# Accumulating layer 0's later modulation groups on VectorE instead of TensorE

## The chip, the core and the metric

The kernel runs on one core of a Trainium2 chip: TensorE (PE), VectorE (DVE), ScalarE (ACT), GpSimd (POOL), and SyncE (SP), which issues the DMA transfers. The metric is the device time of one execution in microseconds.

## What is computed

A backbone of two layers runs over 256 context and 256 latent tokens of width 1024, all in float32. Each layer begins by making six modulation vectors for each of the two streams from a conditioning vector and a 1024 x 6144 matrix. This is the part that the change touches:

```python
c_act = jax.nn.silu(c)
cc_act = jax.nn.silu(c_ctx)
for l in range(DEPTH):
    m_l = jnp.split((c_act @ w_ada[l] + b_ada[l])[:, None, :], 6, axis=-1)
    m_c = jnp.split((cc_act @ w_ada[l] + b_ada[l])[None, None, :], 6, axis=-1)
    h_l = modulate(rms_norm(x, norm_g[l, 0]), m_l[0], m_l[1])
    h_c = modulate(rms_norm(ctx, norm_g[l, 0]), m_c[0], m_c[1])
    y_l, y_c = token_mixer(h_l, h_c, ...)
    x = x + m_l[2] * rms_norm(y_l, norm_g[l, 1])
    h_l = modulate(rms_norm(x, norm_g[l, 2]), m_l[3], m_l[4])
    x = x + m_l[5] * rms_norm(sq_relu_mlp(h_l, w_mlp_up[l], w_mlp_down[l]), norm_g[l, 3])
    ...
```

The token mixer has three branches: a gated linear recurrence (four heads), differential attention (four heads) and windowed attention; each is projected, gated and summed. The product of a vector with w_ada is small arithmetic (two rows), but w_ada is 25 MB per layer and has to pass through some engine.

## The kernel before

Activations are kept transposed in `h`, as a high and a low part in fp32r; each weight block (512 KB twice) is loaded into a ring `raw`, and `weights` (L196) splits it: ScalarE copies the high part (L226), VectorE subtracts it for the low part (L227), into one of two buffers `whl`. A block is consumed by three dense matmuls for each tile (L248 to L250 with tokens as the stationary side, L260 to L262 with weights). At the end of each `weights` call `self.pump(self.rate)` (L229) takes that many closures off the list `pumps` and runs them: this is how the modulation work is spread among the weight blocks.

The six vectors of a layer are computed in three groups of 2048 columns. Group 0 of layer 0 is needed at once and is done at the start, in `first_blocks` (L535). Groups 1 and 2 of layer 0 are queued by `ada_queue`: 16 steps for each group, in which one slice of w_ada, 128 rows by 1024 columns (half of each of four strips), is loaded and multiplied on TensorE by `CA`, which holds both streams in a stationary tile of 32 columns. Four matmuls (L364) go to four column strips of the array and accumulate over eight steps in PSUM bank 7, which is kept for that. `ada_done` (L428) copies the bank out (L433), transposes it (L437) and adds the bias (L443). Layer 1's groups are computed in another way, by `ada_late` while layer 0's MLP runs: VectorE multiplies each slice by its per-partition factor and accumulates it in SBUF, one accumulator per stream (L400, L403); after eight slices TensorE sums over the partitions by four matmuls with `ones` per stream (L412), and the result is copied (L417), transposed (L420) and given its bias (L426).

What sets the order: the program is recorded in source order, and a scheduler with its own timeline places the instructions on each engine's queue; splits and evacuations have high priority, closures run at ordinary priority behind the last weight load (`issue_after`). Each engine's queue then keeps its order. PSUM has eight banks: two for dense outputs (`dps`), the others in rotation for the rest (`mps`), without bank 7 in layer 0's mixers. The helper names in the rows: L795 to L869 are the recurrence heads, L949 to L1036 the differential-attention heads (L949 and L950 scores, L989 to L995 their normalisation on VectorE, L1001 transposes, L1014 values), L1087 to L1122 the windowed attention. The buffers named `arf` are units of 512 columns in one arena.

Of the kernel before, what the change touches and what calls it, by code (L numbers as in the profile page):

```python
# [14 lines left out]
ALU = mybir.AluOpType  # L15
# [96 lines left out]
class Net:  # L112
    def __init__(self, ctx, tc, ins, out):
# [40 lines left out]
        self.rate = 1  # L154
# [198 lines left out]
    def ada_queue(self, l, g):  # L353
        for half in range(2):
            for k in range(8):
                self.pumps.append(lambda half=half, k=k: self.ada_step(l, g, half, k))
        self.pumps.append(lambda: self.ada_done(l, g))

    def ada_step(self, l, g, half, k):
        nc = self.nc  # L360
        ca = self.CA.rearrange("p (k m) -> p k m", m=32)
        raw = self.ada_load(l, g, half, k)
        for j in range(4):
            nc.tensor.matmul(self.ps[7][32 * j:32 * j + 32, half * 256:half * 256 + 256], ca[:, k, :],  # L364
                             raw[:, j * 256:(j + 1) * 256], start=k == 0, stop=k == 7)
        raw.free()

    def ada_late(self, l, groups, ahead=2):

        todo = [(g, half, k) for g in groups for half in range(2) for k in range(8)]  # L370
        raws, acc = [], []

        def step(n):
            while len(raws) < min(n + 1 + ahead, len(todo)):
                raws.append(self.ada_load(l, *todo[len(raws)]))
            g, half, k = todo[n]
            self.ada_acc(raws[n], k, acc, 1 if l == DEPTH - 1 and g else 2)
            if k == 7:
                self.ada_sum(l, g, half, acc)
                acc.clear()  # L380

        self.pumps += [lambda n=n: step(n) for n in range(len(todo))]

    def ada_load(self, l, g, half, k):
        src = self.I["w_ada"][l][k * 128:k * 128 + 128, g * 2048:(g + 1) * 2048]
        src = src.rearrange("p (j h c) -> p j h c", j=4, h=2)[:, :, half, :]
        raw = self.A.get(2)
        with self.tc.issue_after(self.last_dma.ins):
            self.nc.sync.dma_start(raw[:, :].rearrange("p (j c) -> p j c", j=4), src)
        return raw  # L390

    def ada_acc(self, raw, k, acc, streams):

        ca = self.CA.rearrange("p (k m) -> p k m", m=32)
        if k == 0:
            acc += [self.A.get(2) for _ in range(streams)]
# [10 lines left out]
    def ada_sum(self, l, g, half, acc):  # L407
        nc = self.nc
        ps = self.mps()
        for s, a in enumerate(acc):  # L410
            for j in range(4):
                nc.tensor.matmul(ps[32 * j:32 * j + 32, s * 256:s * 256 + 256], self.ones[:, 0:32],  # L412
                                 a[:, j * 256:j * 256 + 256], start=True, stop=True)
            a.free()
        t = self.A.get(1)
        n = 2 * len(acc)
# [5 lines left out]
        qs = slice(2 * half, 2 * half + 2)  # L422
        out = self.M[l].rearrange("p (s g j q) -> p s g j q", s=2, g=3, j=4)[:, :, g, :, qs]
        bb = self.bT[:, l * 48 + g * 16:l * 48 + g * 16 + 16].rearrange("p (j q) -> p j q", j=4)[:, :, qs]
        for s in range(len(acc)):
            nc.vector.tensor_tensor(out=out[:, s], in0=view(p2, s * 256, [(32, 4), (128, 2)]), in1=bb, op=ALU.add)  # L426
# [253 lines left out]
    def hgrn_dense(self, l, w, hp):  # L680
# [560 lines left out]
    def layer(self, l):  # L1241
# [140 lines left out]
    def build(self):  # L1382
        self.setup()
        for g in (1, 2):
            self.ada_queue(0, g)
# [30 lines left out]
```

## Time and profile before

| | |
|---|---|
| median of 3 runs | 1603.66 us (1602.57 to 1603.8) |
| the profiled execution | 1602.47 us, its span 1600.7 us |
| TensorE matmul, weight load | busy 97%, 83% of the span |
| VectorE, ScalarE, GpSimd | busy 65%, 49%, 25% |
| DMA | 220.06 MB, 137 GB/s on average |

The page gives busy time by engine over the whole span; the views below cut the span in stretches, follow single instructions on one engine in order of time, or group instructions by source line. A matmul's end is modelled, so the distance from start to start tells what a matmul costs its engine, and busy time tells more than it takes. Each fp32 matmul appears as two records.

### The profile page before, as it was taken

Reading aid. Unit: us, or ns where it says so; the run is one execution under the profiler, and the core shown is the slowest. Engines: PE = TensorE matmul, PEld = TensorE weight load, DVE = VectorE, ACT = ScalarE, POOL = GpSimd, SP = SyncE. Lnnn points to the kernel's source line nnn. Section 1 sums busy time; section 2 is a strip of 40 time slices with the busy share of each in tenths; the row PEclk is TensorE's granted clock in tenths of the full one; section 3 lists DMA queues with packets and bytes.
Section 4 is the critical chain, followed back from the end, with each engine's and each line's share of the span. In section 5 each row is a group of like instructions: output and inputs, shape, how many; then the busy total and the mean of one; then the engine's idle time right before and its main releaser. Section 6 shows DMA issues by size and latency. Waiting matters only on the chain.

```text
span 1600.7 us, 26956 instructions
## 1 busy us (share of the span) xinstructions
PE 1546.6 (97%) x10326; PEld 1323.4 (83%) x10326; DVE 1045.6 (65%) x1897; ACT 777.4 (49%) x1588; POOL 393.0 (25%) x419
## 2 busy tenths in 40 slices
PE   6999999999999999999999999999898999989997
PEld 4788887878777778888888888999897999889996
DVE  3655544577477568777656546786668788665665
ACT  4443433446444457533424246644445656666553
POOL 1142415050420001210102011464455250121001
PEclk9999999999999999999999999999999999999999
DMA  9823234233332336466566434432334254446562
GB/s 282 236 80 119 75 114 143 80 79 115 123 93 79 115 109 211 140 202 194 176 208 191 151 106 145 125 114 78 122 106 106 67 149 125 148 139 191 185 185 92
DMA packets 209681, 220.06 MB, mean 137 GB/s; under 512 B 24400, under 2 KB 177168, under 8 KB 209552
## 3 DMA queue, kind: packets, MB, share of 16 engines
q1 hardware_dynamic: 209552, 218.34, 45.2%
q8 instruction: 81, 1.33, 0.3%
q14 instruction: 48, 0.39, 0.1%
HBM read 217.26 MB, written 1.05 MB: 136 GB/s over the span
## 4 chain that ended last, share of the span: by engine, by line
PE 85%; DVE 5%; POOL 4%; DMA 2%; ACT 2%; issue 2%; SPq 1%; POOLq 0%; DVEq 0%; ACTq 0%
PE b L248 16%; PE b L249 16%; PE b L250 16%; PE b L260 8%; PE b L261 8%; PE b L262 8%; POOL arf L919 1%; PE b L364 1%; DVE whl L227 1%; PE b L1122 1%; PE b L1109 1%; PE b L869 1%; PE b L949 1%; PE b L950 1%; PE b L853 1%
## 5 line engine op out<-in xcount | busy, mean ns | idle before, releaser
L227 DVE TENSOR_TENSOR whl<-raw,whl 128x512 fp32r<-128x512 f32 x588 | 431.4, 753 | 243.3 <-ACT whl L226 233.7
L226 ACT CAST whl<-raw 128x512 fp32r<-128x512 f32 x588 | 356.3, 620 | 256.4 <-PE b L262 129.3
L248 PE MATMUL b<-h,whl 128*128 128x512 f32 (+1 forms) x1296 | 447.6, 347 | 1.2 <-ACT arf L964 0.6
L250 PE MATMUL b<-h,whl 128*128 128x512 f32 (+1 forms) x1296 | 444.9, 344 | 0.8 <-DVE whl L227 0.8
L249 PE MATMUL b<-h,whl 128*128 128x512 f32 (+1 forms) x1296 | 444.6, 343 | 0.4 <-POOL h L606 0.3
L248 PEld LDWEIGHTS b<-h,whl 128*128 128x128 f32 x1296 | 247.9, 192 | 33.8 <-ACT whl L226 2.9
L250 PEld LDWEIGHTS b<-h,whl 128*128 128x128 f32 x1296 | 246.8, 191 | 29.5 <-issue 1.6
L249 PEld LDWEIGHTS b<-h,whl 128*128 128x128 f32 x1296 | 246.9, 191 | 28.9 <-issue 2.4
L1332 POOL TENSOR_TENSOR arf<-arf 128x256 f32<-128x256 f32 (+1 forms) x68 | 59.8, 880 | 411.3 <-ACT arr L1331 399.5
L262 PE MATMUL b<-whl,arr 128*128 128x512 f32 x384 | 149.9, 390 | 0.0
L261 PE MATMUL b<-whl,arr 128*128 128x512 f32 x384 | 149.9, 390 | 0.0
L260 PE MATMUL b<-whl,arr 128*128 128x512 f32 x384 | 149.7, 391 | 0.0
L919 POOL TENSOR_TENSOR arf<-arf,cst 32x256 f32<-32x256 f32 x104 | 94.3, 907 | 192.3 <-ACT arf L964 70.7
L260 PE MATMUL b<-whl,h 128*128 128x256 f32 (+1 forms) x416 | 129.0, 313 | 0.0
L261 PE MATMUL b<-whl,h 128*128 128x256 f32 (+1 forms) x416 | 128.7, 311 | 0.0
L262 PE MATMUL b<-whl,h 128*128 128x256 f32 (+1 forms) x416 | 128.6, 311 | 0.0
L455 POOL TENSOR_TENSOR sm<-sm,nhalf 128x1 f32<-128x1 f32 (+2 forms) x42 | 37.0, 883 | 333.5 <-DVE sm L630 242.5
L809 POOL TENSOR_TENSOR arf<-arf 128x512 f32<-128x512 f32 x56 | 75.8, 1376 | 43.7 <-ACT arf L788 24.1
L260 PEld LDWEIGHTS b<-whl,h 128*128 128x128 f32 x416 | 80.0, 192 | 6.4 <-ACT arf L753 0.8
L260 PEld LDWEIGHTS b<-whl,arr 128*128 128x128 f32 x384 | 72.1, 188 | 15.9 <-issue 1.2
L262 PEld LDWEIGHTS b<-whl,arr 128*128 128x128 f32 x384 | 72.1, 188 | 14.9
L261 PEld LDWEIGHTS b<-whl,arr 128*128 128x128 f32 x384 | 72.1, 188 | 14.5
(224 smaller groups left out, 2434.1 us busy)
## 6 DMA issues: line engine op xcount, KB each, us to landing
raw<-in_w_in_dram SPq DMA_DIRECT2D x110, 512.0 KB, 3.9
arf<-in_w_ada_dram SPq DMA_DIRECT2D x80, 512.0 KB, 4.9
raw<-in_w_mlp_down_dram SPq DMA_DIRECT2D x72, 512.0 KB, 3.8
raw<-in_w_mlp_up_dram SPq DMA_DIRECT2D x64, 512.0 KB, 4.3
raw<-in_w_out_dram SPq DMA_DIRECT2D x24, 512.0 KB, 4.2
arf<-in_w_ada_dram SPq DMA_DIRECT2D x32, 256.0 KB, 5.6
raw<-in_w_branch_dram SPq DMA_DIRECT2D x16, 512.0 KB, 3.9
raw<-in_w_in_dram SPq DMA_DIRECT2D x32, 128.0 KB, 3.3
```

The costliest lines, as they stand in the source:

```text
L226: self.behind(ops, lambda: nc.scalar.copy(r32(h), src))
L227: self.split_op = self.behind(ops, lambda: nc.vector.tensor_tensor(out=r32(l), in0=src, in1=h, op=ALU.subtract))
L248: nc.tensor.matmul(ps, wh, xh[:, t0:t0 + n], start=start and k == 0, stop=False)
L249: nc.tensor.matmul(ps, wh, xl[:, t0:t0 + n], start=False, stop=False)
L250: nc.tensor.matmul(ps, wl, xh[:, t0:t0 + n], start=False, stop=stop and k == nk - 1)
L260: nc.tensor.matmul(ps, xh, wh, start=start and k == 0, stop=False)
L261: nc.tensor.matmul(ps, xh, wl, start=False, stop=False)
L262: nc.tensor.matmul(ps, xl, wh, start=False, stop=stop and k == nk - 1)
L455: self.nc.gpsimd.tensor_tensor(out=r, in0=ms, in1=self.nhalf[:, 0:cols], op=ALU.pow)
L809: nc.gpsimd.tensor_tensor(out=kx, in0=kx, in1=view(cur, 1, [(nb - 1, 2), (2, nb // 2), (0, h)]), op=ALU.mult)
L919: nc.gpsimd.tensor_tensor(out=b[o, 0:LAT], in0=x[i], in1=self.cst[i, C_RS:C_RS + LAT], op=ALU.mult)
L1332: nc.gpsimd.tensor_tensor(out=r[:, c], in0=r[:, c], in1=r[:, c], op=ALU.mult)
```

## The change

Layer 0's groups 1 and 2 now go through `ada_late` too, in quarters of 512 columns; two closures run per weight block instead of one, so that the same 1024 columns pass per block. `ada_queue` and `ada_step` are gone. Bank 7 joins the rotation after `first_blocks`. Layer 1's slices, still 1024 columns, are now consecutive columns instead of half of each strip.

```diff
-        self.rate = 1
+        self.rate = 2
...
-    def ada_queue(self, l, g):
-        for half in range(2):
-            for k in range(8):
-                self.pumps.append(lambda half=half, k=k: self.ada_step(l, g, half, k))
-        self.pumps.append(lambda: self.ada_done(l, g))
-
-    def ada_step(self, l, g, half, k):
...
-        raw = self.ada_load(l, g, half, k)
-        for j in range(4):
-            nc.tensor.matmul(self.ps[7][32 * j:32 * j + 32, half * 256:half * 256 + 256], ca[:, k, :],
-                             raw[:, j * 256:(j + 1) * 256], start=k == 0, stop=k == 7)
...
-    def ada_late(self, l, groups, ahead=2):
+    def ada_late(self, l, groups, cols, ahead=2):
 
-        todo = [(g, half, k) for g in groups for half in range(2) for k in range(8)]
+        todo = [(g, c0, k) for g in groups for c0 in range(0, 2048, cols) for k in range(8)]
         raws, acc = [], []
 
         def step(n):
             while len(raws) < min(n + 1 + ahead, len(todo)):
-                raws.append(self.ada_load(l, *todo[len(raws)]))
+                raws.append(self.ada_load(l, cols, *todo[len(raws)]))
...
-    def ada_load(self, l, g, half, k):
-        src = self.I["w_ada"][l][k * 128:k * 128 + 128, g * 2048:(g + 1) * 2048]
-        src = src.rearrange("p (j h c) -> p j h c", j=4, h=2)[:, :, half, :]
-        raw = self.A.get(2)
+    def ada_load(self, l, cols, g, c0, k):
+        c0 += g * 2048
+        raw = self.A.get(cols // UNIT)
         with self.tc.issue_after(self.last_dma.ins):
-            self.nc.sync.dma_start(raw[:, :].rearrange("p (j c) -> p j c", j=4), src)
+            self.nc.sync.dma_start(raw[:, :], self.I["w_ada"][l][k * 128:k * 128 + 128, c0:c0 + cols])
...
-    def ada_sum(self, l, g, half, acc):
+    def ada_sum(self, l, c0, cols, acc):
+
         nc = self.nc
         ps = self.mps()
+        w, nb = cols // 4, cols // 512
         for s, a in enumerate(acc):
             for j in range(4):
-                nc.tensor.matmul(ps[32 * j:32 * j + 32, s * 256:s * 256 + 256], self.ones[:, 0:32],
-                                 a[:, j * 256:j * 256 + 256], start=True, stop=True)
+                nc.tensor.matmul(ps[32 * j:32 * j + 32, s * w:s * w + w], self.ones[:, 0:32],
+                                 a[:, j * w:j * w + w], start=True, stop=True)
             a.free()
         t = self.A.get(1)
-        n = 2 * len(acc)
+        n = nb * len(acc)
...
+            self.np = 8
             self.setup_mixers()
...
-            self.ada_late(1, range(3))
+            self.ada_late(1, range(3), 1024)
             self.rate = 0
...
-        for g in (1, 2):
-            self.ada_queue(0, g)
+        self.ada_late(0, (1, 2), 512)
```

How the order moves. In the changed kernel the lines lie 13 to 16 lower: L387 and L384 are the former L403 and L400, L398 the former L412, L406 the former L420, L936, L937, L976, L982, L988 and L1001 the former L949, L950, L989, L995, L1001 and L1014, L840 and L856 the former L853 and L869.

The first place is TensorE at the end of the recurrence of layer 0's first head pair. Before:

```order
L853 MATMUL b_86<-arf 128x256 x4
L869 MATMUL b_88<-arf 128x128 x2
L869 MATMUL b_87<-arf 128x128 x6
L869 MATMUL b_88<-arf 128x128 x3
L364 MATMUL b_91<-arf,CA 32x256 x3
L869 MATMUL b_88<-arf 128x128 x6
L364 MATMUL b_91<-arf,CA 32x256 x9
L249 MATMUL b_85<-h,whl 128x512
```

and in the changed kernel:

```order
L840 MATMUL b_86<-arf 128x256 x4
L856 MATMUL b_87<-arf 128x128 x2
L856 MATMUL b_88<-arf 128x128 x4
L856 MATMUL b_87<-arf 128x128 x6
L856 MATMUL b_88<-arf 128x128 x7
L398 MATMUL b_91<-arf,ones 32x128 x8
L248 MATMUL b_85<-h,whl 128x512
```

The steps of four matmuls with 256 columns are gone, and the first of the eight sums, with 128 columns, stands there instead.

The second place is VectorE in the middle of the differential attention. Before, while the heads run:

```order
L992 RECIPROCAL sm<-sm 128x2
L993 TENSOR_SCALAR arf<-arf,sm,lam 128x512
L995 SCALAR_TENSOR_TENSOR arf<-arf,sm 128x512
L992 RECIPROCAL sm<-sm 128x2
L993 TENSOR_SCALAR arf<-arf,sm,lam 128x512
L227 TENSOR_TENSOR whl<-raw,whl 128x512
L995 SCALAR_TENSOR_TENSOR arf<-arf,sm 128x512
L227 TENSOR_TENSOR whl<-raw,whl 128x512
```

and in the changed kernel, at the change from the first head pair to the second:

```order
L976 TENSOR_REDUCE sm<-b_90 128x1
L917 TENSOR_TENSOR arr<-arf,arr 64x512
L387 SCALAR_TENSOR_TENSOR arf<-arf,CA 128x512
L976 TENSOR_REDUCE sm<-b_89 128x1
L982 SCALAR_TENSOR_TENSOR arf<-arf,sm 128x512
L387 SCALAR_TENSOR_TENSOR arf<-arf,CA 128x512
L979 RECIPROCAL sm<-sm 128x2
L917 TENSOR_TENSOR arr<-arf,arr 64x512
L980 TENSOR_SCALAR arf<-arf,sm,lam 128x512
```

The accumulations (L387) stand between the steps of a head's normalisation; 17 of the 128 new VectorE instructions lie between the first L976 and the last L982 of layer 0.

The third place is TensorE towards the end of the same heads. Before:

```order
L248 MATMUL b_84<-h,whl 128x512
L249 MATMUL b_84<-h,whl 128x512
L949 MATMUL b_88<-arr 128x512
L950 MATMUL b_88<-arr 128x512
L250 MATMUL b_84<-h,whl 128x512
L949 MATMUL b_89<-arr 128x512
L1001 MATMUL b_90<-cst,arf 128x128 x4
L950 MATMUL b_89<-arr 128x512
L248 MATMUL b_84<-h,whl 128x512
L249 MATMUL b_84<-h,whl 128x512
```

and in the changed kernel:

```order
L988 MATMUL b_89<-cst,arf 128x128 x2
L936 MATMUL b_88<-arr 128x512
L937 MATMUL b_88<-arr 128x512
L936 MATMUL b_86<-arr 128x512
L937 MATMUL b_86<-arr 128x512
L936 MATMUL b_87<-arr 128x512
L937 MATMUL b_87<-arr 128x512
L1001 MATMUL b_91<-arf 128x128 x4
L936 MATMUL b_88<-arr 128x512
L937 MATMUL b_88<-arr 128x512
L1001 MATMUL b_86<-arf 128x128 x2
```

The dense matmuls that stood between the heads' steps there now stand behind them: from layer 0's first scores to the last transposes of its heads the order has 340 dense matmuls, and 391 before.

## Rows read from the trace of the kernel before

**Rows 1.** The page, part 1: busy us, share of the span, instructions, by engine.

```profile
PE 1546.6 (97%) x10326; PEld 1323.4 (83%) x10326; DVE 1045.6 (65%) x1897; ACT 777.4 (49%) x1588; POOL 393.0 (25%) x419
```

**Rows 2.** The page, part 4: shares of the chain that ended last, by engine.

```profile
PE 85%; DVE 5%; POOL 4%; DMA 2%; ACT 2%; issue 2%; SPq 1%; POOLq 0%; DVEq 0%; ACTq 0%
```

**Rows 3.** Stretches (us): length; PE, PEld, DVE, ACT, POOL busy; clock; DMA; GB/s.

```profile
50.00:600.00 550.00, 542.91 (x3829) 441.54 (x3819) 332.23 (x666) 245.32 (x510) 133.13 (x142) 1.00 0.37 108
289.00:404.00 115.00, 111.19 (x619) 93.05 (x618) 81.88 (x159) 57.43 (x136) 23.15 (x26) 0.99 0.35 95
```

**Rows 4.** Waits of TensorE, 50 to 600 us: total us, times, longest.

```profile
PE b L795 <- DVE arf L812: 2.7, 4, 1.2
PE b L364 <- DMA arf<-in_w_ada_dram: 1.5, 2, 1.3
```

**Rows 5.** Timeline of TensorE: start, length (us), line, tile, records.

```profile
71.37 0.39 PE L249 MATMUL b<-h,arr 128*128 128x512 f32 x1
71.59 0.39 PE L250 MATMUL b<-h,arr 128*128 128x512 f32 x1
71.91 0.64 PE L364 MATMUL b<-arf,CA 128*32 128x256 f32 x8
72.48 0.39 PE L260 MATMUL b<-whl,h 128*128 128x256 f32 x1
72.70 0.28 PE L261 MATMUL b<-whl,h 128*128 128x256 f32 x1
```

**Rows 6.** TensorE by line: records, busy us, mean ns, idle before.

```profile
L364 PE MATMUL b<-arf,CA 128*32 128x256 f32 x256 | 23.3, 390 | 1.5 <-DMA arf<-in_w_ada_dram 1.5
...
L412 PE MATMUL b<-arf,ones 128*32 128x256 f32 x64 | 4.7, 388 | 0.0
```

**Rows 7.** Timeline of TensorE at a step of group 0.

```profile
30.70 0.40 PE L248 MATMUL b<-h,whl 128*128 128x512 f32 x1
31.02 0.64 PE L535 MATMUL b<-arf,CA 128*32 128x128 f32 x16
31.60 0.50 PE L249 MATMUL b<-h,whl 128*128 128x512 f32 x1
31.93 0.39 PE L250 MATMUL b<-h,whl 128*128 128x512 f32 x1
```

**Rows 8.** Timeline of TensorE at the transposes of ada_done.

```profile
357.64 0.60 PE L437 MATMUL b<-cst,arf 128*128 128x128 f32 x4
357.99 0.37 PE L260 MATMUL b<-whl,h 128*128 128x256 f32 x1
```

**Rows 9.** VectorE by line, the accumulation of layer 1.

```profile
L403 DVE SCALAR_TENSOR_TENSOR arf<-arf,CA 128x1024 f32<-128x1024 f32 x56 | 76.3, 1385 | 3.5 <-DMA arf<-in_w_ada_dram 3.0
...
L400 DVE TENSOR_SCALAR arf<-arf,CA 128x1024 f32<-128x1024 f32 x8 | 5.9, 748 | 1.5 <-DMA arf<-in_w_ada_dram 1.5
```

**Rows 10.** VectorE by line, 289 to 404 us.

```profile
L227 DVE TENSOR_TENSOR whl<-raw,whl 128x512 fp32r<-128x512 f32 x28 | 19.1, 704 | 3.4 <-ACT whl L226 3.3
L989 DVE TENSOR_REDUCE sm<-b 128x1 f32<-128x512 f32 x16 | 10.6, 684 | 8.7 <-PE b L950 8.5
...
L995 DVE SCALAR_TENSOR_TENSOR arf<-arf,sm 128x512 f32<-128x512 f32 x8 | 7.1, 881 | 0.2
...
L993 DVE TENSOR_SCALAR arf<-arf,sm,lam 128x512 f32<-128x512 f32 x8 | 4.9, 614 | 0.2
```

**Rows 11.** Waits of VectorE, 289 to 404 us.

```profile
DVE sm L992 <- ACT arf L910: 4.0, 8, 1.0
DVE whl L227 <- ACT whl L226: 3.3, 3, 1.3
```

**Rows 12.** Single microseconds, columns as in Rows 3.

```profile
328.00:329.00 1.00, 0.37 (x3) 0.25 (x2) 1.00 (x4) 1.00 (x5) 0.17 (x1) 1.00 0.00 0
330.00:331.00 1.00, 1.00 (x4) 0.81 (x3) 1.00 (x1) 0.00 (x0) 0.94 (x2) 0.50 0.00 0
```

**Rows 13.** Waits of SP's queue, 50 to 600 us.

```profile
SPq L217 <- DVE whl L227: 320.5, 55, 16.5
```

More of the change, by code (lines that the diff above doesn't have):

```diff
@@ L351, in pump @@
                 self.pumps.pop(0)()
-    def ada_queue(self, l, g):
-        for half in range(2):
-            for k in range(8):
-                self.pumps.append(lambda half=half, k=k: self.ada_step(l, g, half, k))
-        self.pumps.append(lambda: self.ada_done(l, g))
-    def ada_step(self, l, g, half, k):
-        nc = self.nc
-        ca = self.CA.rearrange("p (k m) -> p k m", m=32)
-        raw = self.ada_load(l, g, half, k)
-        for j in range(4):
-            nc.tensor.matmul(self.ps[7][32 * j:32 * j + 32, half * 256:half * 256 + 256], ca[:, k, :],
-                             raw[:, j * 256:(j + 1) * 256], start=k == 0, stop=k == 7)
-        raw.free()
-    def ada_late(self, l, groups, ahead=2):
-        todo = [(g, half, k) for g in groups for half in range(2) for k in range(8)]
+    def ada_late(self, l, groups, cols, ahead=2):
+        todo = [(g, c0, k) for g in groups for c0 in range(0, 2048, cols) for k in range(8)]
         raws, acc = [], []
@@ L374, in step @@
             while len(raws) < min(n + 1 + ahead, len(todo)):
-                raws.append(self.ada_load(l, *todo[len(raws)]))
-            g, half, k = todo[n]
+                raws.append(self.ada_load(l, cols, *todo[len(raws)]))
+            g, c0, k = todo[n]
             self.ada_acc(raws[n], k, acc, 1 if l == DEPTH - 1 and g else 2)
             if k == 7:
-                self.ada_sum(l, g, half, acc)
+                self.ada_sum(l, g * 2048 + c0, cols, acc)
                 acc.clear()
         self.pumps += [lambda n=n: step(n) for n in range(len(todo))]
-    def ada_load(self, l, g, half, k):
-        src = self.I["w_ada"][l][k * 128:k * 128 + 128, g * 2048:(g + 1) * 2048]
-        src = src.rearrange("p (j h c) -> p j h c", j=4, h=2)[:, :, half, :]
-        raw = self.A.get(2)
+    def ada_load(self, l, cols, g, c0, k):
+        c0 += g * 2048
+        raw = self.A.get(cols // UNIT)
         with self.tc.issue_after(self.last_dma.ins):
-            self.nc.sync.dma_start(raw[:, :].rearrange("p (j c) -> p j c", j=4), src)
+            self.nc.sync.dma_start(raw[:, :], self.I["w_ada"][l][k * 128:k * 128 + 128, c0:c0 + cols])
         return raw
@@ L395, in ada_acc @@
         if k == 0:
-            acc += [self.A.get(2) for _ in range(streams)]
+            acc += [self.A.get(raw.k) for _ in range(streams)]
         for s, a in enumerate(acc):
@@ L421, in ada_sum @@
         t.free()
-        qs = slice(2 * half, 2 * half + 2)
-        out = self.M[l].rearrange("p (s g j q) -> p s g j q", s=2, g=3, j=4)[:, :, g, :, qs]
-        bb = self.bT[:, l * 48 + g * 16:l * 48 + g * 16 + 16].rearrange("p (j q) -> p j q", j=4)[:, :, qs]
+        i = c0 // 128
         for s in range(len(acc)):
-            nc.vector.tensor_tensor(out=out[:, s], in0=view(p2, s * 256, [(32, 4), (128, 2)]), in1=bb, op=ALU.add)
+            out = self.M[l][:, s * 48 + i:s * 48 + i + 4 * nb].rearrange("p (j q) -> p j q", j=4)
+            bb = self.bT[:, l * 48 + i:l * 48 + i + 4 * nb].rearrange("p (j q) -> p j q", j=4)
+            nc.vector.tensor_tensor(out=out, in0=view(p2, s * w, [(32, 4), (128, nb)]), in1=bb, op=ALU.add)
     def ada_done(self, l, g, qs=range(4), p2=None):
```

## The prediction

> **What bounds the kernel now.** I read the page's busy shares first: TensorE 97%, its weight loads 83%, VectorE 65% [rows 1]. Busy is not the same as limiting, so the second look is the chain that ended last: 85% of it lies on TensorE [rows 2]. The third is the stage that the change touches, from 50 us, where layer 0's first matmuls run, to 600 us, where its mixers end. There TensorE is busy 542.91 of 550 us, VectorE 332.23 [rows 3]. TensorE's own waits name what it lacked: the longest is 2.7 us for VectorE at L812, and 1.5 us go to the w_ada loads in front of L364 [rows 4]; with five smaller ones they make the 7.0 us that are left. So in this stage time is what TensorE has to issue, and a microsecond off its queue is a microsecond off the end, as long as its suppliers keep up. VectorE, with 218 us idle there, looks like the place with room; whether the room lies where it is needed is the question of this case.
>
> **What the removed matmuls cost.** The mean of one L364 record, 390 ns, is no price: 256 records (128 matmuls, two records each) are busy for only 23.3 us together [rows 6], because four column strips overlap. Start to start shows it: L250 starts at 71.59, the eight records of one step at 71.91, the next dense matmul at 72.48 and the one after at 72.70 [rows 5]. Dense neighbours of 512 columns start 0.22 apart, of 256 columns 0.12. One step thus inserts 72.48 - 71.59 - 0.23 = 0.66 us, and 0.10 more in the slow first dense step behind it: 0.76 us, of which 0.57 is the step and 0.19 the way in and out. With 32 steps that is 18.2 us (all joined to other fp32 work) to 24.3 us (all alone); most stand alone, I take 23. Their DMA waits go too: 1.5 us [rows 4]. The two closing helpers (ada_done) each put four transposes on TensorE, 0.35 us [rows 8] and 0.19 for the way in and out: 1.1 together. **Removed: 25.6 us.**
>
> **What TensorE gets instead.** Eight sums, one for each quarter of 512 columns of two groups, each of eight matmuls with 128 columns and `ones`, then two transposes. The first stage has the same shape: eight L535 matmuls (16 records) start at 31.02, the next dense one at 31.60; the way in is 0.32 instead of 0.23, the way out 0.33 [rows 7]. That is 0.58 + 0.19 = 0.77 for a sum; the order shows two of the eight cut in two, 0.4 more: 6.6 us. The dearest row near it, L412 with twice the columns, 64 records for 4.7 us [rows 6], would make 1.2 for a sum and 9.4 in all. Two transposes are half of the 0.35 [rows 8] and again 0.19: 0.37, eight times 3.0. **Added: 9.6 us (up to 12.4). Net on TensorE: 16.0 us less** (between 18.2 + 2.6 - 12.4 = 8 and 24.3 + 2.6 - 9.6 = 17).
>
> **What VectorE gets.** 64 steps of two streams: 16 first products and 112 accumulations of 512 columns. The accumulation exists in the trace only at 1024 columns, 1.385 us, and the first product at 0.748 [rows 9]. Half of the first, 0.69, is one bound; the same kind of instruction at 512 columns (L995, 0.881) the other; the split at L227, equally 512 columns from two SBUF tiles, takes 0.704 [rows 10], and I take 0.70: 79 us. The first product lies between 0.37 and 0.75; at 0.45, 16 make 7 us. Together 86 us (83 to 111), and VectorE's share of the stage rises from 60% to about 79%.
> [...]
>
> **Where VectorE could be late.** Between 289 and 404 us the four differential-attention heads run. VectorE is busy 81.88 of these 115 us [rows 3] and waits 7.3 more for ScalarE [rows 11]. Seventeen new instructions stand there in its order (15 x 0.70 + 2 x 0.45 = 11.4): it needs about 100 us. TensorE needs 111.2 - 2.3 for three removed steps, but the order has 51 fewer dense matmuls in front of the last head's transposes (51 x 0.23 = 11.6 us, which run later): 97 us. So VectorE, which had slack here, becomes about equal. At the very end twelve TensorE rows stand without a dense matmul. A 512-column unit asks VectorE for two reductions, a division, L993 and L995, 2 x 0.684 + 0.614 + 0.881 = 2.9 us [rows 10], and four such units close the stretch: 11.5 us, against some 7 us of TensorE's own work there. Bounds for the stall: 0, if VectorE comes with a lead, and 12, if both amounts (3 and 5) are lost, another accumulation pair falls in front of each, and the clock drops. That last cost is visible already: after TensorE was idle for most of 328 to 329 us, the granted clock was 0.50, the lower level, in the microsecond from 330 [rows 12], which costs about 1.4 us in the 512-column steps there. I take 3 us for all waits.
>
> **What costs nothing.** Behind each weight block the order puts four accumulations, about 2.8 us, beside four splits, 2.8 us; a block keeps TensorE for 48 x 0.227 = 10.9 us, and weights lie ready ahead of it: SP waits 320 us in this stage for buffers that the splits free [rows 13]. The same hides the 32 additional loads on SP; if that cover went, TensorE would wait for weights, which is the slower case below. The new accumulations wait for w_ada data; queued behind them are the splits of the next block, and for those TensorE waits. The loads stand one block (some 11 us) ahead. The sixth PSUM bank for the mixers and the plain column order of layer 1's slices take off or add no instruction of note; both change small places in the order, plus or minus 2 us.
>
> **Sum.** 1602.47 (the profiled execution) - 16 + 3 = 1589.5. That execution lies 1.2 below the median of the runs shown, so as a median **1591**.
>
> **The rivals.** (a) *VectorE sets the pace, slower than before.* Accumulations stand ahead of the next splits in a queue that keeps its order; if each of 32 blocks came late by more than (16 + 3.2) / 32 = 0.6 us, less than one accumulation, the gain would be gone. At 0.7 late with two or three clock drops it ends at 1602.5 - 16 + 22 + 3 = 1611. For it: four accumulations per block. Against it: about 20% of VectorE's time stays free, and blocks are split well ahead. 7%. (b) *No change: TensorE was not full.* If the removed steps lay in time in which TensorE would have waited anyway, for VectorE or for weights, waits of 13 to 19 us take their place: 1601 to 1607. Against it: dense steps start 0.22 apart right up to and behind a step [rows 5]. 8%. [...] (c) *Most of the gain is eaten* in the attention stretch and at the new sums: 9 to 13 us of waits, 1598 to 1600.4. 8%. (d) *More than the sum*: the waits of 7.0 us go as well, through the additional bank and looser loads: 1580 to 1583. 7%.
>
> **How the numbers follow.** The forecast, 1583 to 1598, has 70%. A measurement of this kernel can tell about 0.2%, 3.2 us. Faster by more than that: 70 + 8 + 7 = 85%; within it 8%; slower 7%. The range takes the forecast, case (c) and a little of (d): 1582 to 1600.
>
> **What would show it.** Right: the L364 group is gone, the sums together take 6 to 9 us, dense starts keep 0.22, VectorE is busy some 420 us between 50 and 585. Wrong: waits of TensorE on L995, L227 or an accumulation above 5 us; a granted clock below 1 in the attention stretch for several us; a removed step worth less than 0.6 us.

## The result: slower by 30 us

The changed kernel takes **1633.51 us** (1629.06 to 1634.47), the kernel before, beside it on the same chip, 1603.62: a ratio of 1.018, 95% interval 1.0167 to 1.0193. The prediction was 1591, range 1582 to 1600: wrong in sign, and outside the range.

The page of the kernel after, its busy shares and the chain that ended last, answer to [rows 1] and [rows 2]:

```profile
PE 1545.3 (95%) x10206; PEld 1333.4 (82%) x10206; DVE 1146.7 (70%) x2043; ACT 776.9 (48%) x1588; POOL 406.4 (25%) x419
...
PE 82%; DVE 7%; POOL 6%; issue 2%; ACT 1%; DMA 1%; SPq 1%; POOLq 0%; DVEq 0%; ACTq 0%
```

TensorE has 120 records less and is busy 1.3 us less; the span is 30 us longer. By busy time alone the 30 us are time in which it stood; the account below shows that its work became less and some of its steps slower. The place follows from the stretches of the changed stage; it now ends 30 us later, at 630. Columns as in [rows 3], the same two stretches:

```profile
50.00:630.00 580.00, 541.52 (x3723) 452.74 (x3722) 432.22 (x811) 245.02 (x509) 146.72 (x142) 0.96 0.34 102
303.00:422.00 119.00, 110.90 (x624) 93.70 (x623) 104.98 (x199) 57.82 (x136) 27.81 (x28) 0.96 0.34 96
```

Idle time of TensorE in the stage was 550.00 - 542.91 = 7.1 us and is 580.00 - 541.52 = 38.5: 31 us more, and only 8.1 of the 38.5 lie in the stretch of the attention heads (119.00 - 110.90). VectorE's extra 100 us of work lie within the forecast's bounds (432 busy for "some 420"). The granted clock fell from 1.00 to 0.96 as a mean of the stage. What TensorE waited for, 50 to 630 us (total us, times, longest); the changed kernel's line numbers are 13 to 16 below those of before, so L799 here is L812 there, L982 is L995, and L387 is the accumulation:

```profile
PE b L782 <- DVE arf L799: 12.1, 5, 5.0
PE b L988 <- DVE arf L982: 5.3, 1, 5.3
PE b L936 <- DVE arr L917: 3.7, 2, 3.4
PE b L1096 <- DVE arf L1089: 2.7, 1, 2.7
PE b L248 <- DVE arf L1167: 2.7, 1, 2.7
PE b L936 <- ACT arr L928: 2.2, 1, 2.2
```

In [rows 4] the first of these was 2.7 us. No wait of TensorE on the accumulation itself, or on the splits (L227), is among them: what comes late are the steps of the HGRN levels (L799; HGRN is the gated linear recurrence, which each head works out in levels, one after the other), of the attention heads (L982, L917) and of the sliding-window units (L1089).

**TensorE's account.** From the timelines, as in the prediction, I summed the times from one start to the next by line, without the waits. For 50 to 600 us before and 50 to 630 after, they make 542.8 and 542.2 us. In this: the L364 steps, 20.9 us, are gone; the sums and their transposes (L398, L406) cost 6.4; and 14.6 us were added on instructions that nobody changed, 3.5 of them on 64 matmuls of the top two HGRN levels (L798, now L785: 7.0 to 10.5 us) and 2.1 on the levels below (L795, now L782). The place is visible in single microseconds: within a 5.0 us wait that begins at 114.5 us the granted clock falls to 0.50, the lower of the two levels that the traces of before and after show (0.50 and 1.00), and it stays there into dense work, up to 127:

```profile
117.00:118.00 1.00, 0.00 (x0) 0.00 (x0) 0.88 (x2) 0.68 (x3) 1.00 (x2) 0.50 0.22 46
...
125.00:126.00 1.00, 1.00 (x6) 1.00 (x6) 0.00 (x0) 0.00 (x0) 0.00 (x0) 0.50 0.73 235
128.00:129.00 1.00, 1.00 (x6) 0.80 (x6) 1.00 (x3) 0.16 (x1) 0.96 (x2) 1.00 0.31 51
```

In the changed kernel's stage, 50 to 630 us, the clock is at 0.50 for 51.2 us in seven stretches, each of which begins within a wait of 1.4 us or more or less than 1 us behind it; in the kernel before, 50 to 600 us, for 3.4 us in one. In the kernel before, dense matmuls of 512 columns start 0.43 us apart at 0.50 (329.4 to 332.4 us) and 0.23 at 1.00 (333 to 334.5).

So: -20.9 - 0.7 (ada_done) + 6.4 = -15.2 us of work, close to the -16.0 forecast (which has 1.5 us of DMA waits in it), and against it +31 of waits and +15 of slower steps behind them. The question of this study is where these 46 us come from; the prediction had 3.

**Where it is lost.** To place it, I matched the dense matmuls of 256 and 512 columns of each kernel with those of before, line by line and in sequence, and took the lateness in us, as the median over the 30 us of the kernel before that begin at each of five times. The table, worked out from the timelines, has the main experiments below as well; the HGRN heads lie before 290 us, the differential attention between 289 and 404, so that the column of 420 (420 to 450 us) has some of what lies behind it as well.

| kernel | 90 | 150 | 300 | 420 | 600 |
|---|---|---|---|---|---|
| after | 2.9 | 8.2 | 18.5 | 18.5 | 30.3 |
| before, 4 buffers held (e5) | 0.7 | 8.9 | 16.9 | 23.3 | 32.1 |
| before, 2 buffers held (e12) | 1.3 | 5.7 | 11.4 | 14.7 | 17.1 |
| before, 28 steps left out (e7) | -1.9 | -5.2 | -6.8 | -13.4 | -19.5 |
| after, short accumulations (e1) | -0.8 | 8.2 | 16.7 | 11.8 | 18.8 |
| after, own buffers (e10) | 3.1 | 4.0 | -1.2 | 13.7 | 13.6 |
| own buffers, short (e13) | -0.1 | 0.4 | -5.8 | -2.7 | -8.2 |
| placed (e15) | 3.2 | 4.1 | 7.6 | 8.4 | 6.2 |
| mixed (e17) | 0.9 | 4.6 | 3.5 | 1.4 | 6.7 |

In the changed kernel the lateness stays at 30.3 to 30.6 up to 1380 us. Layer 1's new column order, part of the same diff, costs and gains nothing.

### The profile page after: what moved, and what is told of

Read it like the earlier page. It is cut to its first block, busy times and chain, and to the rows that moved or that the text cites. A ratio compares the mean times of both kernels' runs of the same rounds, so it can differ in the third digit from the quotient of the medians.

```text
span 1630.9 us, 26955 instructions
## 1 busy us (share of the span) xinstructions
PE 1545.3 (95%) x10206; PEld 1333.4 (82%) x10206; DVE 1146.7 (70%) x2043; ACT 776.9 (48%) x1588; POOL 406.4 (25%) x419
## 4 chain that ended last, share of the span: by engine, by line
PE 82%; DVE 7%; POOL 6%; issue 2%; ACT 1%; DMA 1%; SPq 1%; POOLq 0%; DVEq 0%; ACTq 0%
PE b L248 15%; PE b L249 15%; PE b L250 15%; PE b L260 9%; PE b L261 9%; PE b L262 9%; POOL arf L906 2%; POOL arf L796 1%; PE b L1096 1%; PE b L1109 1%; DVE whl L227 1%; PE b L856 1%; PE b L936 1%; PE b L937 1%; PE b L785 1%
## 5 line engine op out<-in xcount | busy, mean ns | idle before, releaser
L227 DVE TENSOR_TENSOR whl<-raw,whl 128x512 fp32r<-128x512 f32 x588 | 431.4, 754 | 240.2 <-ACT whl L226 236.1
L226 ACT CAST whl<-raw 128x512 fp32r<-128x512 f32 x588 | 356.0, 620 | 260.7 <-PE b L262 131.2
L387 DVE SCALAR_TENSOR_TENSOR arf<-arf,CA 128x512 f32<-128x512 f32 (+1 forms) x168 | 167.9, 1028 | 14.4 <-DMA arf<-in_w_ada_dram 13.4
L906 POOL TENSOR_TENSOR arf<-arf,cst 32x256 f32<-32x256 f32 x104 | 98.5, 948 | 199.3 <-PE b L1001 66.8
L897 ACT ACTIVATE arf<-b,sm 128x512 f32<-128x512 f32 (+1 forms) x96 | 58.9, 617 | 59.6 <-DVE sm L976 35.4
L260 PEld LDWEIGHTS b<-whl,arr 128*128 128x128 f32 x384 | 72.1, 188 | 15.8 <-issue 1.2
```

The costliest lines, as they stand in the source:

```text
L226: self.behind(ops, lambda: nc.scalar.copy(r32(h), src))
L227: self.split_op = self.behind(ops, lambda: nc.vector.tensor_tensor(out=r32(l), in0=src, in1=h, op=ALU.subtract))
L260: nc.tensor.matmul(ps, xh, wh, start=start and k == 0, stop=False)
L387: self.nc.vector.scalar_tensor_tensor(out=a[:, :], in0=raw[:, :], scalar=ca[:, k, s:s + 1], in1=a[:, :], op0=ALU.mult, op1=ALU.add)
L906: nc.gpsimd.tensor_tensor(out=b[o, 0:LAT], in0=x[i], in1=self.cst[i, C_RS:C_RS + LAT], op=ALU.mult)
```

## The experiments

The theories at the start: **V**, VectorE's 90 us of accumulations stand in front of what TensorE waits for; **D**, VectorE is held up by late w_ada slices and passes that on (12.1 us of waits of L387 for DMA in the trace); **B**, the sixth PSUM bank upset the order. Later came **A**, the buffers, and **O**, the planned order without the removed steps (the planner is the scheduler that places the instructions on the queues).

### First: amount, data, bank, dose

**e1_short.**

```
-        ca = self.CA.rearrange("p (k m) -> p k m", m=32)
+        ca, n = self.CA.rearrange("p (k m) -> p k m", m=32), 16 if raw.k == 1 else 1024
...
-    scalar_tensor_tensor(out=a[:, :], in0=raw[:, :], ... in1=a[:, :], ...)
+    scalar_tensor_tensor(out=a[:, 0:n], in0=raw[:, 0:n], ... in1=a[:, 0:n], ...)
```

> The changed kernel, but each of layer 0's 112 accumulations works on 16 columns instead of 512 (the other 496 columns of each are left out, so the vectors are not complete); loads, waits for data, sums and transposes all stay. Theory V (VectorE's time: the accumulations, 90 us in the trace, stand in front of the steps that TensorE waits for): the waits of 31 us and the slower steps behind them go, the 15 us taken off TensorE stay, 1583 to 1592 us. Theory D (VectorE is held up by late w_ada slices, 12 us, and passes that on): the waits for data stay, 1612 to 1630. Theory B (the sixth PSUM bank of the mixers upset the order): 1625 to 1635.

Measured: 1623.24 us, ratio 1.0123 (1.0094 to 1.0153), above V's range and inside D's, which the next run settles. Two thirds of the loss stay with the accumulations busy 29 us instead of 90, and TensorE's longest wait, 50 to 620 us, stays where it was. The wait of the attention heads, 5.3 us in the changed kernel, is nearly gone:

```profile
PE b L782 <- DVE arf L799: 8.9, 3, 5.9
PE b L248 <- DVE arf L1167: 3.8, 3, 2.1
PE b L782 <- ACT arf L775: 3.5, 1, 3.5
...
PE b L988 <- DVE arf L982: 0.2, 1, 0.2
```

VectorE's time alone is not the cause.

**e2_ahead4.** `self.ada_late(0, (1, 2), 512)` becomes `self.ada_late(0, (1, 2), 512, 4)`.

> The changed kernel with layer 0's w_ada slices loaded four steps ahead of their accumulation instead of two, nothing left out. Theory D: VectorE's 12 us of waits for w_ada nearly go, and with them at least as much of the time, 1612 to 1622. Theory V: VectorE has as much to do, and only a few us come back, 1624 to 1634.

Measured: 1643.28, ratio 1.0248 (1.0219 to 1.0278): 10 us *slower* than the change, which no theory had. VectorE's waits for w_ada fell from 12.1 to 3.6 us, as D wanted, and yet TensorE's waits for the HGRN steps grew:

```profile
PE b L782 <- DVE arf L799: 16.2, 10, 4.1
```

D falls. What reading further ahead takes instead is two more buffers of 512 columns; this run pointed at them.

**e3_np7.** `self.np = 8` behind the first blocks is taken out.

> The changed kernel with five PSUM banks for the mixers as before the change (the eighth stays unused). Theory B: back to 1590 to 1605. Theories V and D: 1628 to 1640, no better than the change, perhaps some us worse since one bank less decouples the engines.

Measured: 1631.95, ratio 1.0178 (1.0148 to 1.0207). B falls: the bank makes no more than 2 us.

**e4_g2_vec.** Group 1 through before's `ada_queue` and `ada_step`, then `self.ada_late(0, (2,), 512)` with two steps per call.

> Half the change: group 1 accumulates on TensorE as before the change (one step of 1024 columns per weight block), group 2 on VectorE in quarters (two steps per block) behind it; five banks for the mixers. Theory V, with the loss spread evenly over the mixers: half of it, 1612 to 1620. If the loss is that of the HGRN heads (up to 290 us), which this leaves nearly free: 1600 to 1608. If it is that of the attention stages: 1616 to 1626.

Measured: 1626.17, ratio 1.0142 (1.0112 to 1.0171). Half the dose costs three quarters. By lateness it is even with before up to 300 us (-0.6), and loses 22 between there and 600, which fits the forecast for a loss in the attention stages (the time is at its upper end): each stage has a loss of its own.

### Second: the buffers

Both raw slices and sums come from one pool of 33 buffers of 512 columns, out of which the mixers take all their tiles; the pool gives the one freed longest ago. Counted in the program's own sequence, the TensorE steps kept two of them for a moment each; the new code keeps two slices and two sums from one step to the next, four all the time (the expectations below count the most within one step: five, and two before). Counted in the same sequence, at the narrowest place of the HGRN heads the next tile is taken from 9 free buffers instead of 13.

**e5_hold4**, the test of this alone, on the kernel before:

```
+            self.idle = [self.A.get(1) for _ in range(4)]      # behind setup_mixers()
...
+            [t.free() for t in self.idle]                      # behind layer 0's mixers
```

> The kernel before with one thing added: four of the 33 buffers of 512 columns are taken before layer 0's mixers and given back behind them, and nobody uses them. TensorE's and VectorE's work is that of before. Theory A (buffers: the sums in the making and the slices read ahead keep five buffers where the TensorE steps kept two for a short time, so the mixers' tiles come round sooner and the order bunches the HGRN levels): 1612 to 1632 us. Theory V (VectorE's time): 1601 to 1607, no change.

Measured: **1635.55 us, ratio 1.0193** (1.0147 to 1.0239), a little above A's range and far from V's. Four buffers that nobody uses cost as much as the whole change, with all of TensorE's steps still there and no accumulation on VectorE, and they leave the same 9 at the narrowest place. Its stretches, columns as in [rows 3], and its first waits:

```profile
50.00:300.00 250.00, 236.10 (x2150) 199.59 (x2150) 135.38 (x229) 90.11 (x161) 84.76 (x84) 0.96 0.35 110
300.00:420.00 120.00, 115.60 (x628) 95.12 (x627) 81.05 (x161) 60.17 (x140) 20.60 (x26) 0.97 0.26 75
```

```profile
PE b L795 <- DVE arf L812: 13.1, 5, 5.7
PE b L1001 <- DVE arf L995: 1.8, 2, 1.4
```

The wait of TensorE on L812, 2.7 us in [rows 4], is 13.1 with the buffers gone, as it is 12.1 in the changed kernel. How it comes about is to be read on ScalarE, whose L788 (L775 in the changed kernel) copies a new tile for each HGRN level, 14 of them for a pair of heads. In the kernel before, five of them are still to come at 100 us; they are done when the next weight block is to be cast (start, length, line, tile, idle before it; the first row is one of the earlier nine):

```profile
91.74 0.62 ACT L788 COPY arf<-arf 128x512 f32<-128x512 f32 x1 [0.55 <-DVE arf L729]
...
102.62 0.62 ACT L788 COPY arf<-arf 128x512 f32<-128x512 f32 x1 [2.04 <-POOL arf L809]
104.11 0.63 ACT L788 COPY arf<-arf 128x512 f32<-128x512 f32 x1 [0.87 <-POOL arf L809]
105.15 0.62 ACT L788 COPY arf<-arf 128x512 f32<-128x512 f32 x1 [0.41 <-POOL arf L809]
106.62 0.62 ACT L788 COPY arf<-arf 128x512 f32<-128x512 f32 x1 [0.85 <-POOL arf L809]
108.09 0.62 ACT L788 COPY arf<-arf 128x512 f32<-128x512 f32 x1 [0.84 <-POOL arf L809]
108.62 1.66 ACT L226 CAST whl<-raw 128x512 fp32r<-128x512 f32 x3
```

With four buffers held, eleven are still to come at 100 us, and the last of them stand between the casts of that block (L226), some of them waiting for GpSimd (the first row is one of the earlier three):

```profile
85.79 0.88 ACT L788 COPY arf<-arf 128x512 f32<-128x512 f32 x1
...
109.88 0.62 ACT L788 COPY arf<-arf 128x512 f32<-128x512 f32 x1 [0.45 <-POOL arf L809]
110.92 0.62 ACT L788 COPY arf<-arf 128x512 f32<-128x512 f32 x1 [0.42 <-POOL arf L809]
111.45 0.62 ACT L226 CAST whl<-raw 128x512 fp32r<-128x512 f32 x1
111.97 0.61 ACT L788 COPY arf<-arf 128x512 f32<-128x512 f32 x1
112.49 0.61 ACT L226 CAST whl<-raw 128x512 fp32r<-128x512 f32 x1
113.01 0.61 ACT L788 COPY arf<-arf 128x512 f32<-128x512 f32 x1
113.53 0.61 ACT L226 CAST whl<-raw 128x512 fp32r<-128x512 f32 x1
114.44 0.62 ACT L788 COPY arf<-arf 128x512 f32<-128x512 f32 x1 [0.29 <-POOL arf L809]
```

The three casts start at 111.45 instead of 108.62 and end at 114.14 instead of 110.28; the levels (the chain through L809 on GpSimd and L812 on VectorE) have lost their lead, so TensorE has neither the next dense block nor the next level. What held the copies back is ScalarE's own order: between the casts at 84.56 and 95.17 of the kernel before four of them stand in its queue (two at 85.08, then 88.86 and 91.74), between the same casts with four buffers held, at 85.27 and 95.87, only the one at 85.79, though ScalarE is idle there three times for 2.0 to 2.8 us. Where the section on the change has TensorE's planned order at the end of this head pair, the traces show the same one (in the changed kernel 38 records of L856 in a row, two for each matmul, then 16 of L398). Taking the same of ScalarE, which was not shown, it was the planner that placed them behind. The changed kernel shows the same at the same place, three dense matmuls and then 5 us of nothing:

```profile
112.83 0.76 PE L782 MATMUL b<-arf 128*32 128x32 f32 x64
113.52 0.50 PE L248 MATMUL b<-h,whl 128*128 128x512 f32 x1
113.86 0.40 PE L249 MATMUL b<-h,whl 128*128 128x512 f32 x1
114.09 0.40 PE L250 MATMUL b<-h,whl 128*128 128x512 f32 x1
119.52 0.66 PE L782 MATMUL b<-arf 128*32 128x32 f32 x32 [5.04 <-DVE arf L799]
```

**e7_no_steps**, the removal alone, on the kernel before: `for j in range(4)` becomes `for j in range(4 if k == 0 else 0)`.

> The kernel before with 28 of the 32 TensorE steps left out (the first of each half group stays, so the vectors are not complete); the loads stay, nothing goes to VectorE, no buffer is kept longer. Theory A, and my term of 0.76 us for a step: 28 x 0.76 = 21 us less and up to 1.5 of DMA waits, 1579 to 1584. Theory O (the removed steps were TensorE's cover, and without them the planned order itself gets worse): 1590 to 1605.

Measured: 1585.13, ratio 0.9878 (0.9833 to 0.9924), 18.1 us less for 28 steps: 0.65 us for one, all included (the interval allows 12 to 27 us, 0.44 to 0.96 for one). It lies 1 us above A's range and below O's. O falls: the work removed here from TensorE was worth what it lasted (20.9 us for 32 steps in the account above, 0.65 for one as well).

**e6_own2** and **e8_own1**: two buffers for the sums out of the other pool, `nf, nr, ne = 33, 20, 2`, a pool E of its own for `acc`; e8 also reads one slice ahead instead of two.

> The changed kernel with two buffers of their own for layer 0's sums in the making (two of the 22 buffers of the other pool, which are never all in use), so the mixers' pool lends out three buffers instead of five. Theory A: at least a third of the 46 us comes back, 1600 to 1616. Theory V: VectorE does the same work, 1626 to 1634.

> As the kernel with two buffers of its own for the sums, and one slice read ahead instead of two: the mixers' pool lends out two buffers, as many as before the change. Theory A: most of the loss is gone, 1590 to 1604. Theory D (late slices hold VectorE up): later than with two slices ahead, 1610 to 1630. Theory V: 1626 to 1634.

Measured: 1628.28 (ratio 1.0147, 1.0101 to 1.0193) and 1616.63 (1.0069, 1.0037 to 1.0102). Both miss A's ranges: 1628.28 lies in V's, 1616.63 in D's, though D had it later than own2. Two buffers fewer brought 5 us, three fewer 17. In the right direction; but own1, which lends about as few as the kernel before, ends 13 us above it, where TensorE's account has it 15 below.

**e9_before35** and **e12_hold2**: the dose, on the kernel before (`nf, nr = 35, 20`; two idle buffers instead of four).

> The kernel before with 35 buffers of 512 columns in the mixers' pool instead of 33 (two are taken from the other pool of 22, whose last two are never used in layer 0 or 1). Theory A, if the time falls steadily with free buffers: 4 to 10 us less, 1593 to 1600. Theory A with a step (below about 33 it hurts, above nothing is gained): 1601 to 1606.

> The kernel before with two idle buffers held through layer 0's mixers instead of four. Theory A, steady: between 1603 and 1635, 1612 to 1626. Theory A with a step between 33 and 29: either 1601 to 1607 or 1630 to 1637.

Measured: 1607.06 (1.0024, 1.0013 to 1.0036) with two more, 1622.43 (1.0115, 1.0094 to 1.0137) with two fewer. From 35 over 33, 31 and 29 buffers: 1607, 1604, 1622, 1636. More than 33 gain nothing: 1607 is above both forecasts, and its 3 us show what another dealing of the tiles alone can do to the time. Below 33, the first two cost 9 us each (e12 lies inside its steady forecast) and the next two 7.

**e10_own4**, nothing lent: a pool E of four (two from the other pool, two from the weights' ring, `RAWS = 4`), one slice ahead.

> The changed kernel with four buffers of its own for sums and slices (one slice read ahead); two come from the other pool, two from the weights' ring, which has four half blocks instead of five. The mixers' pool of 33 is lent to nobody. Theory A: TensorE's 15 us are gained at last, 1586 to 1597. If VectorE's time (90 us) or the shorter ring costs as well: 1598 to 1612. Theory V: above 1615.

Measured: 1614.27 (1.0064, 1.0044 to 1.0085), outside all three ranges. Up to 300 us A holds: the loss is nearly gone (-1.2 in the table; without any loss it would be near the -6.8 of e7). Behind it A fails: 15 us are lost between the columns of 300 and 420, so the forecast of A alone missed by 17. Some 8 of the 15 are lost by 410 us; behind the heads come waits of 3.1 us on L874 and 2.2 on an accumulation that a sum needs.

**e11_psum**: the sums in PSUM banks 6 and 7, `acc += [self.ps[6 + i] ...]`, copied out by ScalarE.

> The changed kernel with the two sums of a quarter accumulated in PSUM banks 6 and 7 (four banks are left to the mixers), copied by ScalarE to SBUF for TensorE's last step; the slices have two buffers of their own from the other pool, one read ahead. The mixers' pool lends out nothing but two buffers for a moment per quarter. Theory A: 1588 to 1600. If VectorE's time or the lost banks cost as well: 1600 to 1615.

Measured: 1633.24 (1.0183, 1.0159 to 1.0206), far above both ranges. In the HGRN heads it is as good as own4 was in the first pair and 7 us worse at 300 (5.9), then it loses 32 in the attention stages, where TensorE's longest wait in total is one on ScalarE's exponentials (10.3 us). Two banks and ScalarE's copies were taken there; which of them did it was not tried.

### Third: VectorE's time after all

**e13_own4_short**, the edit of e1_short in own4.

> The kernel with four buffers of its own, each of layer 0's 112 accumulations on 16 columns instead of 512 (the other 496 columns of each are left out, so the vectors are not complete). Theory V2 (with the buffers out of the way, VectorE's time is the rest): 1585 to 1595, 19 to 29 us below own4. If it is the ring or the planned order: 1606 to 1616.

Measured: **1589.82, ratio 0.9912** (0.989 to 0.9935). With both causes away, the second as far as 16 columns do it, the prediction's sum is there: 13.8 us less than before (10 to 18 by the interval). The attention stretch, own4 above, own4_short below, columns as in [rows 3]:

```profile
300.00:420.00 120.00, 111.46 (x602) 94.35 (x602) 103.14 (x185) 61.82 (x144) 43.38 (x46) 0.91 0.28 80
```

```profile
300.00:420.00 120.00, 111.65 (x623) 94.27 (x622) 103.64 (x204) 65.55 (x149) 49.15 (x54) 0.97 0.29 81
```

VectorE is busy 103 of 120 us in both: in the second it has more of the attention's own work done in that time (by the table it is 5 us ahead of own4 at 300 and 16 at 420). TensorE's idle time is the same in both, 8.5 and 8.4 us; what differs there is the clock, 0.91 against 0.97. In own4 the clock is at its lower level from 322 to 336 us, with three waits of 0.7 to 1.3 us from 321.5 on; own4_short has no such stretch there. The accumulations of the two kernels, busy and mean:

```profile
L387 DVE SCALAR_TENSOR_TENSOR are<-are,CA 128x512 f32<-128x512 f32 x112 | 93.8, 869 | 2.1 <-DMA are<-in_w_ada_dram 1.8
```

```profile
L387 DVE SCALAR_TENSOR_TENSOR are<-are,CA 128x16 f32<-128x16 f32 x112 | 31.9, 329 | 4.0 <-DMA are<-in_w_ada_dram 3.6 <-DVE are L387 0.2
```

62 us less on VectorE are worth 24.5 of the time. The four kernels make a square:

| | 512 columns | 16 columns |
|---|---|---|
| four buffers lent by the mixers' pool | 1633.5 (the change) | 1623.2 (e1) |
| buffers of its own | 1614.3 (e10) | 1589.8 (e13) |

Buffers cost 19 us with VectorE's work there and 33 without most of it; the part of VectorE's work that was left out costs 10 or 24. They do not add up: each hides part of the other.

**e14_before_raws4**, the control for the ring that own4 shortened: `RAWS = 4` in the kernel before.

> The kernel before with four half blocks in the weights' ring instead of five. If the shorter ring is what own4 lost: 1612 to 1630. Theory V2: 1602 to 1608.

Measured: 1604.00 (1.0005, 0.9994 to 1.0015). The ring costs the kernel before nothing; with the change it was not tried alone, but e13 has the shorter ring and reaches the sum.

**e15_placed**: steps per weight block from a list, 34 blocks: `[2]*7 + [4]*4 + [3]*3 + [0]*8 + [2]*6 + [3]*4 + [0]*2`.

> own4 with other numbers of steps per weight block: 2 in the HGRN blocks, 4 and 3 in the gate and first attention blocks behind them, none in the branch, second attention and sliding-window blocks, then 2 and 3 again; the same steps in the same sequence. Theory V2: VectorE is free in the attention stretch, most of the 15 us come back, 1597 to 1606. If the number counts and not the place: 1611 to 1617.

Measured: 1608.68 (1.0035, 1.0023 to 1.0048), 5.6 us less than own4 and between the two ranges. Between 300 and 420 it loses 0.8 instead of 15: V2 is right about the place. It loses 9 elsewhere instead, at 270 us, where four steps per block make the sum on TensorE come before its accumulations (a wait of 4.6 us).

**e16_placed_out**: the last 16 steps go to w_out's blocks, `while len(self.pumps) > 16` at the end of the mixers; the list of steps per block is another one, too, with fewer in the blocks that had 4 and 3.

> As placed, but the last quarter of the steps (the vector that the MLP's end needs) is taken out of the mixers and goes to the blocks of w_out, two per block. Theory V2: another 0 to 5 us, 1593 to 1604; if VectorE is late at w_out, where it does the norms, 1606 to 1618.

Measured: 1621.16 (1.0108, 1.0093 to 1.0123), above both ranges. Up to 600 us it is as late as placed (6.4), then it loses 15 up to 700, the most in one place, an 8.3 us wait of TensorE for the norm's output (L592) on ScalarE; placed has 3.3 us there.

**e17_mixed**: own buffers, 24 + 24 VectorE steps in the blocks that had shown no loss, the last vector in eight TensorE steps.

> Both causes avoided: four buffers of its own as in own4, 48 of the 64 VectorE steps, in the blocks in which own4 and placed lost nothing (24 from the third HGRN block to the first attention block, 24 from the second gate block on, none between); the last vector is accumulated on TensorE, eight steps of 1024 columns in the blocks left out. If buffers and VectorE's time are all: 32 - 8 = 24 TensorE steps of 0.65 less, six sums of 0.8 more, some us of waits, 1592 to 1601, below the kernel before. If something else stands behind the loss: 1604 or more.

Measured: 1606.33 (1.0022, 1.0013 to 1.0031). A miss: 5 us above the range for the two causes, and not below the kernel before; it lies in the range for something else. Its waits, 50 to 620 us (L787 and L804 are the HGRN level and its VectorE step, L941 a matmul of the attention and L902 its exponential):

```profile
PE b L787 <- DVE arf L804: 4.2, 3, 2.8
PE b L941 <- ACT arf L902: 4.2, 5, 2.1
PE b L787 <- ACT arf L780: 2.5, 2, 2.3
```

By the table 4 us are lost in the first HGRN pair, as in own4 and placed (4.0 and 4.1 at 150, where own4_short has 0.4), and 5 between 540 and 580. Every edit of the amounts has the planner set a new order on all engines; that the small losses come from this was not tried by itself. No version here beats the kernel before with its work complete.

## Why the prediction was wrong

**The work on TensorE: right in the net.** Removed: 0.65 us for a step (the account, and e7), where I had 0.76, so with the DMA waits 20.9 + 1.5 us instead of 24.5; the transposes 0.7 for 1.1. Added: 6.4 for eight sums with transposes, 0.80 each, where I had 1.2 and 9.6. Both were about 3 us too high, and in the net the two errors cancel: -16.7 against -16.0. That the net is so close is luck; e13 bears it out as time, -13.8.

**VectorE's amount: right.** The accumulations and first products measure 99 us, inside the 83 to 111:

```profile
L387 DVE SCALAR_TENSOR_TENSOR arf<-arf,CA 128x512 f32<-128x512 f32 x112 | 90.5, 840 | 12.7 <-DMA arf<-in_w_ada_dram 12.1
...
L384 DVE TENSOR_SCALAR arf<-arf,CA 128x512 f32<-128x512 f32 x16 | 8.6, 548 | 2.7 <-PE b L1109 1.4 <-PE b L988 1.1 <-PE b L840 0.2
```

The value taken, 0.70, was low for 0.84.

**The step that failed: "I take 3 us for all waits", with bounds of 0 and 12.** It measured 31 us of waits and 15 of slower steps behind them. Two things are in it.

The larger one is missing from the prediction altogether: the buffers. The part on what costs nothing went through weights, loads, the PSUM bank and the column order, and did not ask what the new steps *keep* while they run. The bound of 12 was made from the rows of one stretch, and from VectorE's work alone; e5 shows 32 us with no such work at all. The view of [rows 13] had a sign of it. Its 320 us are waits for the weights' ring, and e14 shows that this ring is not short. But further down in the same view the loads of w_ada (L389) wait for tiles of the mixers that are still being read, 68 us in eleven rows, of which this is the first:

```profile
SPq L389 <- DVE arf L995: 17.3, 3, 13.4
```

The row doesn't say what that costs; it says that the pool was in use. The tiles of the mixers were never counted.

In the traces of e5 and e12 TensorE's idle time from 50 to 600 us is 22 and 19 us instead of 7.1; in e5 the two longest gaps are 5.7 us at 112 us and 5.1 at 204, one for each pair of HGRN heads; the rest of their 32 and 19 us of time is, by the difference, slower steps (the granted clock is 0.96 to 0.97 in the three stretches 50 to 300, 300 to 420 and 420 to 600 us of e5, and 0.97 in the first of e12). The trace of before had no such gaps to be warned by: its longest in the stage is 1.3 us.

The smaller one was in the prediction, as rival (c) with 8%: VectorE in the differential-attention heads. I had both engines about equal there (100 and 97 us of need) and gave it 3 us. VectorE was busy 105 of 119 us in that stretch and TensorE lost its 5.3 us exactly on the row that I had named (L995, now L982); without the buffers' part, e10 loses 15 us between the columns of 300 and 420 and e13, with 62 us less on VectorE in all, only 3. The balance of 100 and 97 was itself wrong. It took 51 dense matmuls off TensorE, from the 340 that stand beside 391 in the section on the change. Counted in both traces from the first scores to the last transposes of layer 0's heads, the changed kernel has 424 (256 of 512 columns and 168 of 256) and the kernel before 391 (295 and 96), in columns the same to 1%. By the same sum TensorE's need was about 108 us (111.2 - 2.3 - 0.7), above VectorE's 100, and VectorE was late all the same: totals of a stretch did not decide it. So that the wait came on the row named was in part luck.

**The rivals.** (a) comes nearest, slower at 1611, and its condition was wrong: it had the splits of the weights late, and TensorE has no wait on L227 in the stage. (b), that removed steps were worth nothing, is refuted by e7. **What would show it**: "waits on L995, L227 or an accumulation above 5 us" came true for L995; "granted clock below 1 in the attention stretch" came true (0.96 for 0.99).

**What stays open.** How a held buffer makes the order worse was seen at one place, in the first HGRN pair, where ScalarE's copies stand later in its order; that the planner placed them so, because their tiles came free later, is argued, not shown, and at the other places waits on the chip and the planner's order were not separated. Why two buffers less were worth only 5 us in e6 but 19 in e12 is not settled, nor why own4, placed and mixed lost 4 us in the first HGRN pair.

## What to carry to other kernels

Before work moves to an engine with room, count the buffers that it keeps from one step to the next, and what else is fed from that pool: here four of 33, idle, cost as much as the whole change. And idle time of an engine, summed over a stage, is no room: VectorE had 218 us of it in the stage, but 33 in the 115 us of the attention heads (115.00 - 81.88), in which 28 of the 128 new instructions then ran. Test such a change with its parts apart: the removal alone (-18 us), the buffers alone (+32) and the new work made short (-14 with buffers of its own) each took one run.

## What the runs showed of the hardware

The accumulation has a large fixed part: in the changed kernel 512 columns take 736 ns at least (median 746), in e13 16 columns 219 (median 230), so 496 columns cost 0.52 us, and the other 0.2 us is there at either width, an estimate by a straight line through these two widths.

Beside GpSimd, VectorE's L812 took up to twice as long: 1396 ns against 693 at most without it. In the kernel before, L812 with 512 columns, while GpSimd is in L809 and when it is not:

```profile
101.03 9.05 POOL L809 TENSOR_TENSOR arf<-arf 128x512 f32<-128x512 f32 x7
...
101.74 1.39 DVE L812 TENSOR_TENSOR arf<-arf 128x512 f32<-128x512 f32 x1
...
111.75 0.68 DVE L812 TENSOR_TENSOR arf<-arf 128x512 f32<-128x512 f32 x1
```

Of the 28 such L812 in that trace, the 15 that meet no GpSimd instruction take 674 to 693 ns, and the ten that lie wholly beside one 693 to 1396, 1226 in the median. In the rows L812 is 0.71 us longer there; why is not shown, nor what GpSimd loses.

The accumulation's spread goes the same way. In the changed kernel its 112 take 746 ns in the median, 840 in the mean and 1761 at most; the 84 that meet no GpSimd instruction take 736 to 753, and of the 28 that meet one 22 take 1096 to 1761. In e11, where the sums lie in PSUM and of the two tensors only the slice is read from SBUF, all 112 take 739 to 757, though 28 of them meet a GpSimd instruction:

```profile
L387 DVE SCALAR_TENSOR_TENSOR b<-are,CA,b 128x512 f32<-128x512 f32 x112 | 78.6, 748 | 0.9 <-DMA are<-in_w_ada_dram 0.7
```
